# The first feed-forward block in two passes: two of its three token chunks by seven block products in place of eight

## The chip, the cores and the metric

The kernel runs on one core of a Trainium2 chip. The time is the device time of one execution in microseconds, and the figure for a kernel is the median of several runs. A profile is one further execution with the hardware profiler on.

Engines are called as in the profile: PE (matrix products; PEld is its weight load), DVE (vector), ACT (scalar and activations), POOL (general), SP (here only a queue of transfers). Each takes its instructions in program order and waits on semaphores of the others.

## What is computed

One layer of a decoder: a half-step feed-forward block, a mixer of two head groups, and a second feed-forward block. The change touches the first feed-forward block and what joins it to the mixer's projection.

```python
D_MODEL, SEQ, N_META, D_FF = 1024, 1024, 16, 2816

def swiglu(h, w_in, w_out):
    gu = h @ w_in
    g, u = jnp.split(gu, 2, axis=-1)
    return (jax.nn.silu(g) * u) @ w_out

h = h + 0.5 * swiglu(rms_norm(h, ffn1_norm), ffn1_w_in, ffn1_w_out)
u = rms_norm(h, mix_norm) @ w_in
...
h = h + 0.5 * swiglu(rms_norm(h, ffn2_norm), ffn2_w_in, ffn2_w_out)
```

Sixteen meta tokens stand ahead of the 1024 real ones, so the first block has 1040 tokens; the second has 1024.

## The kernel before

**Products.** Everything is float32. To use the fast float32r format, each operand is split into a high part (a cast on ACT: `wh`, `xh`, `ah`, `th`) and a low part (the remainder, a subtraction on DVE or POOL: `wl`, `xl`, `al`, `tl`). Each product of a 128x128 weight tile then takes three PE instructions: high by high, low weight by high, high weight by low.

**The first block** (`ffn`). Tokens are cut into three chunks (`THIRDS`: 352, 344, 344 columns). There are 22 tiles of 128 hidden columns. For each, `stage_in` loads two column tiles of `ffn1_w_in`, splits them, and for each chunk makes `g` and `u` (24 PE instructions each), the gate on ACT (L248), the product on DVE (L249), and its halves `ah` (ACT, L251) and `al` (POOL, L253). `stage_out` takes two hidden tiles at a time, four at the end, and adds their part of the output to `hT` in SBUF (L269). Weights are thus split once for all three chunks, and activations never leave SBUF. Row tiles of x are loaded twice: for the norm (`first_norm`, L622 transposes) and for `hT` (`first_h`). The next norm is made chunk by chunk as `hT` gets ready (`norm_sum`, `inv_rms_rows`, `spread_rows`, `norm_chunk`, from `hooks`). Four projections of the mixer, k and v of the first two chunks, are made at the end beside the norm of the third (`project_early`); k and v of the third follow in `sb_project`.

**The second block** works already in two passes by seven block products, on two chunks of 512 tokens. `fast_in` makes the first pass: for each pair of hidden tiles a "quad" for the gate and one for the other half. A quad multiplies a 2x2 array of weight blocks (128 columns by 512 rows each) with a 2x2 array of token blocks (`B11`, `B21`, `B22`, `T1` to `T4`, made once). The weight combinations are four sums per quad on POOL (L367), and each of the seven weight operands is cast on ACT (L352) and its remainder made on DVE (L354), in three buffers. Results are put together on eviction, and the activations, with their own combinations (POOL, L480, L487), are stored in memory. `fast_out` makes the second pass: for each of seven block products in turn, 11 steps of a weight block of 128x512 and an activation block, both loaded, combined on DVE where needed (L548 to L558) and split (L534, L536), twelve PE instructions each (L582).

**Order.** On PE the order is that of the code (`manual_schedule`). On the other engines and on the queues a scheduler orders instructions by their place in the code and by what they wait for. A tile waits for the last reader of the buffer that it takes.

## Time and profile before

| | us |
|---|---|
| median of 3 runs | 2216.79 (2215.99 to 2218.63) |
| the profiled execution | 2215.04 |
| its span, first to last instruction | 2213.3 |
| first block: first product, last product | 24.1, 813.6 |
| second block, first pass: first and last `qa` | 1547.3, 1973.2 |
| second block, second pass: first and last `o` | 1984.3, 2203.9 |

The page gives busy time by engine, the span in 40 slices, the chain that ended last and the costliest groups. Durations of PE instructions overlap, so the pace of PE is read from starts, or from a count in a stretch of time.

### The profile page before, as it was taken

What the parts mean: (1) busy time and instruction counts of PE and PEld (TensorE: products, weight loads), DVE (VectorE), ACT (ScalarE), POOL (GpSimd) and SP (SyncE); (2) the same over time, 40 slices, a digit from 0 to 9 for tenths busy, and PEclk for the clock granted to TensorE, in tenths of its full rate; (3) what the DMA queues carried; (4) which work ended last, traced back from release to release, by engine and by line L of the source; (5) the groups of instructions that cost most, each with busy time, mean ns of one, the idle gap of its engine ahead of it and who ended that gap; (6) DMA issues with size and microseconds to landing.
All of it is one profiled execution on the core that took longest, in us unless ns stands there. A gap on an engine that the chain in (4) does not pass through costs nothing.

```text
span 2213.3 us, 30720 instructions
## 1 busy us (share of the span) xinstructions
PE 2118.8 (96%) x11916; PEld 1909.2 (86%) x11916; DVE 1179.8 (53%) x1735; ACT 739.1 (33%) x1469; POOL 536.6 (24%) x562
## 2 busy tenths in 40 slices
PE   5999999999999999999999998899899999999999
PEld 4999999999999998997878777787678888878887
DVE  4333223333233163335666659667876767666774
ACT  6311121111211244345555540313423333333443
POOL 1000110011101241233323325211364545440000
PEclk9999999999999999999999999999999999999999
DMA  5311111111111123733433243234533333348363
GB/s 163 106 39 57 39 48 48 39 58 39 57 39 48 46 80 128 208 119 112 123 108 115 87 160 119 73 101 138 160 121 100 106 94 108 97 152 292 112 201 134
DMA packets 215470, 231.08 MB, mean 104 GB/s; under 512 B 18236, under 2 KB 163260, under 8 KB 214812
## 3 DMA queue, kind: packets, MB, share of 16 engines
q1 hardware_dynamic: 203388, 200.47, 29.0%
q0 software_dynamic: 7440, 24.39, 2.9%
q10 hardware_dynamic: 4496, 4.27, 0.6%
q8 instruction: 94, 1.54, 0.3%
q14 instruction: 52, 0.43, 0.1%
HBM read 168.74 MB, written 60.33 MB: 103 GB/s over the span
## 4 chain that ended last, share of the span: by engine, by line
PE 40%; DVE 6%; issue 2%; ACT 2%; POOL 1%; DMA 1%; SPq 0%; DVEq 0%; POOLq 0%; ACTq 0%
PE o L582 9%; PE qb L393 8%; PE qc L393 5%; PE qa L393 5%; PE lvl L779 2%; PE wo L163 1%; PE wo L164 1%; PE wo L162 1%; PE proj L162 1%; DVE keep L1130 1%; PE proj L163 1%; PE proj L164 1%; PE flip L987 1%; DVE attn L788 1%; POOL sig L1133 1%
## 5 line engine op out<-in xcount | busy, mean ns | idle before, releaser
L253 POOL TENSOR_TENSOR al<-sg,ah 128x344 fp32r<-128x344 f32 (+1 forms) x66 | 78.4, 1188 | 655.9 <-ACT ah L251 655.9
L149 DVE TENSOR_TENSOR wl<-raw,wh 128x1024 fp32r<-128x1024 f32 (+1 forms) x112 | 130.7, 1176 | 169.3 <-ACT wh L147 168.0
L147 ACT CAST wh<-raw 128x1024 fp32r<-128x1024 f32 (+1 forms) x112 | 109.4, 986 | 305.8 <-PE o L267 189.0
L162 PE MATMUL proj<-xh,wh 128*128 128x344 f32 (+2 forms) x576 | 205.9, 357 | 1.5 <-ACT wh L147 1.5
L163 PE MATMUL proj<-xh,wl 128*128 128x344 f32 (+2 forms) x576 | 201.1, 349 | 0.8 <-DVE wl L149 0.8
L164 PE MATMUL proj<-xl,wh 128*128 128x344 f32 (+2 forms) x576 | 200.3, 348 | 0.0
L249 DVE TENSOR_TENSOR sg<-sg,u 128x344 f32<-128x344 f32 (+1 forms) x66 | 34.0, 515 | 286.9 <-PE u L164 286.9
L393 PE MATMUL qb<-T,wh 128*128 128x512 f32 x528 | 176.2, 395 | 6.7 <-ACT T L301 3.7
L269 DVE SCALAR_TENSOR_TENSOR hT<-o,hT 128x344 f32<-128x344 f32 (+1 forms) x240 | 123.4, 518 | 101.0 <-PE o L267 101.0
L162 PE MATMUL g<-xh,wh 128*128 128x344 f32 (+1 forms) x528 | 171.5, 325 | 0.0
L163 PE MATMUL g<-xh,wl 128*128 128x344 f32 (+1 forms) x528 | 170.9, 324 | 0.0
L265 PE MATMUL o<-ah,wh 128*128 128x344 f32 (+1 forms) x528 | 170.6, 323 | 0.0
L267 PE MATMUL o<-al,wh 128*128 128x344 f32 (+1 forms) x528 | 170.5, 323 | 0.0
L164 PE MATMUL g<-xl,wh 128*128 128x344 f32 (+1 forms) x528 | 170.1, 322 | 0.0
L266 PE MATMUL o<-ah,wl 128*128 128x344 f32 (+1 forms) x528 | 170.1, 322 | 0.0
L163 PE MATMUL u<-xh,wl 128*128 128x344 f32 (+1 forms) x528 | 169.7, 321 | 0.0
L162 PE MATMUL u<-xh,wh 128*128 128x344 f32 (+1 forms) x528 | 169.4, 321 | 0.0
L164 PE MATMUL u<-xl,wh 128*128 128x344 f32 (+1 forms) x528 | 169.1, 320 | 0.0
L354 DVE TENSOR_TENSOR wl<-s,wh 128x512 fp32r<-128x512 f32 x88 | 123.1, 1400 | 43.1 <-ACT wh L352 42.3
L393 PEld LDWEIGHTS qb<-T,wh 128*128 128x128 f32 x528 | 100.1, 190 | 31.6 <-ACT T L301 4.1
L1133 POOL TENSOR_TENSOR sig<-sig,keep 128x144 f32<-128x144 f32 (+3 forms) x64 | 80.1, 1252 | 178.0 <-DVE keep L1130 114.1
L582 PE MATMUL o<-tl,wh 128*128 128x512 f32 x308 | 120.3, 392 | 2.9 <-DVE tl L536 2.9
(291 smaller groups left out, 5249.7 us busy)
## 6 DMA issues: line engine op xcount, KB each, us to landing
raw<-in_ffn_w_in_dram SPq DMA_DIRECT2D x96, 256.0 KB, 3.0
raw<-in_ffn_w_in_dram SPq DMA_DIRECT2D x44, 512.0 KB, 3.6
raw<-in_ffn_w_out_dram SPq DMA_DIRECT2D x66, 256.0 KB, 4.6
raw<-in_w_in_dram SPq DMA_DIRECT2D x30, 512.0 KB, 3.6
raw<-in_ffn_w_out_dram SPq DMA_DIRECT2D x22, 512.0 KB, 3.6
ks<-kD SPq DMA_DIRECT2D x32, 260.0 KB, 4.6
row<-in_x_dram SPq DMA_DIRECT2D x10, 512.0 KB, 5.1
vD<-vhl SPq DMA_DIRECT2D x8, 512.0 KB, 4.8
```

The costliest lines, as they stand in the source:

```text
L147: nc.scalar.copy(hi, raw)
L149: nc.vector.tensor_sub(lo, raw, hi.bitcast(F32))
L162: nc.tensor.matmul(ps, wh[:, s], xs, start=k == 0, stop=False)
L163: nc.tensor.matmul(ps, wl[:, s], xs, start=False, stop=False)
L164: nc.tensor.matmul(ps, wh[:, s], xl[:, k, c0 : c0 + n], start=False, stop=k == nk - 1)
L265: nc.tensor.matmul(o, wh[:, s], ah, start=i == 0, stop=False)
L266: nc.tensor.matmul(o, wl[:, s], ah, start=False, stop=False)
L267: nc.tensor.matmul(o, wh[:, s], al, start=False, stop=end)
L269: nc.vector.scalar_tensor_tensor(h, o, 0.5, h, ALU.mult, ALU.add)
L354: nc.vector.tensor_sub(lo, src, hi.bitcast(F32))
L393: nc.tensor.matmul(ps, a[:, k, :], b[:, k, :], start=start and k == 0 and i == 0, stop=k == 3 and i == 2, skip_group_check=True,)
L582: nc.tensor.matmul(banks[bank][m], y[:, m * P : (m + 1) * P], z, start=start and q == 0 and e == 0, stop=q == nq - 1 and e == 2, skip_grou ...
```

## The change

The first block now uses `fast_in` and `fast_out` too. Chunks 2 and 1 (344 tokens each) are the two columns of token blocks; chunk 0 (352 tokens) is multiplied plainly.

First pass: for the first three pairs of hidden tiles the plain chunk goes first, 96 PE instructions per pair, while chunks 2 and 1 are loaded (on POOL's queue), normed, transposed and combined (`first_plain`, `first_block`, `first_combined`). Then the seven block products of these three pairs follow, and for the other eight pairs both together: the plain products (`alone`) use weight operands while these are there for the block products, with one operand more (`also`). Between quads two row tiles at a time of x are transposed and stored as `xD` (`turn_x`).

Second pass: 22 steps of the plain chunk with all eight output tiles (`plain_round`), with the loads of `hT` from `xD` after the fourth, then the seven block products. The norm of chunk 0 is spread over the steps of A12 and A11, that of chunk 1 over S3 and A22, that of chunk 2 over A22 and six early projections. `ffn`, `norm_sum`, `norm_chunk`, `first_norm` and `first_h` are gone.

```diff
+    def fast_in(self, ops, n, w_in, actD, openers, ev0, open_ev, feed=None, plain=None,
+                between=lambda: None):
...
+            if also:
+                yield operand(a21)
...
+        def alone(ps, w, h, start):
+            if start:
+                ps = pin.tile([P, n0], F32, tag="qd", name="qd", bufs=2)
+            times(ps, w, plain, 4 * h, start)
+            return ps
+        def plain_quad(col, take):
+            for i in range(2):
+                ps = None
+                for h in range(2):
+                    ps = alone(ps, operand(block(i, h, col)), h, h == 0)
+                take(i, ps)
...
                 p1 = first()
+                if also:
+                    d = alone(None, last[0], 0, True)
                 u2 = kept("u2", p1, go("b", "T2", True))
                 take(0, 0, go("a", "B21", False), None)
+                if also:
+                    also(0, alone(d, last[0], 1, False))
...
+        if plain:
+            for f in ahead:
+                gate, up = plain_pair(f)
+                plain_quad(f * P, gate)
+                yield
+                plain_quad(D_FF + f * P, up)
+                yield
+            ev["p"] = open_ev()
+            for f in ahead:
+                for q in pair(f):
+                    drain(q)
+                    between()
...
+        def plain_round():
+            c0, n0 = plain
...
+            for f in range(D_FF // P):
+                ws = [halved(raw(i, f % 2, f // 2), "w", 512) for i in range(2)]
+                xh, xl = halved(right(f, n0), "t", n0)
+                for m in range(KT):
...
+                if f == 3:
+                    load_h()
+            for m in range(KT):
+                h = hT[:, m, c0 : c0 + n0]
+                nc.vector.scalar_tensor_tensor(h, ps[m], 0.5, h, ALU.mult, ALU.add)
+            ready("plain")
...
+    def first_block(self, ci, rows, junk, pool, name, ops):
...
+        self.norm_rows(ci, rows, junk)
...
+            nc.scalar.mul(t, ps, self.g1[:, k : k + 1])
+            got.append(t)
+            if ops:
+                self.halve(ops[("B11", "B21")[k // 4]], t, k % 4)
...
+                    self.first_plain(rows[0], junk, plain)
+                    next(steps)
+                    next(steps)
+                    ba = self.first_block(2, rows[1], junk, rp, "ba", ops)
+                    next(steps)
+                    next(steps)
+                    bb = self.first_block(1, rows[2], junk, rp, "bb", None)
+                    made = self.first_combined(ba, bb, ops, rp, nw)
...
+                    def load_h():
+                        for k in range(KT):
+                            nc.sync.dma_start(hT[:, k, :], xD[k])
...
+                    self.ring_bufs = 5
...
+                    project_early("k", wk, 0, self.pproj)
+                    project_early("v", wv, 0, pe)
+                    next(last)
+                    project_early("k", wk, 1, self.pproj)
+                    next(last)
+                    project_early("v", wv, 1, pe)
+                    drain(last)
+                    project_early("k", wk, 2, pe)
+                    project_early("v", wv, 2, pe)
```

DVE in the steady part of the first block, before; a row is line, operation, output and inputs, shape, and how often in a row:

```order
L149 TENSOR_TENSOR wl<-raw,wh 128x1024
L249 TENSOR_TENSOR sg<-sg,u 128x352
L249 TENSOR_TENSOR sg<-sg,u 128x344
L149 TENSOR_TENSOR wl<-raw,wh 128x1024
L249 TENSOR_TENSOR sg<-sg,u 128x344
L269 SCALAR_TENSOR_TENSOR hT<-o,hT 128x352
L149 TENSOR_TENSOR wl<-raw,wh 128x1024
L269 SCALAR_TENSOR_TENSOR hT<-o,hT 128x352 x7
L269 SCALAR_TENSOR_TENSOR hT<-o,hT 128x344 x16
```

DVE in the first pass now, in the second quad of a pair that has the plain chunk (`sp` is that chunk's activation, `u` and `sg` those of the block products, `qa` to `qd` PSUM banks):

```order
L397 TENSOR_TENSOR sp<-qd,sp 128x352
L278 TENSOR_TENSOR wl<-raw,wh 128x512
L361 TENSOR_TENSOR u_2353<-qb,p_2265 128x344
L278 TENSOR_TENSOR wl<-s,wh 128x512
L426 TENSOR_TENSOR u<-qc,u_2353 128x344
L427 TENSOR_TENSOR sg<-u,sg 128x344
L278 TENSOR_TENSOR wl<-raw,wh 128x512
L426 TENSOR_TENSOR u<-qb,p_2265 128x344
L427 TENSOR_TENSOR sg<-u,sg 128x344
L278 TENSOR_TENSOR wl<-raw,wh 128x512
```

Each weight remainder is now half as long and serves one or two products of twelve instructions instead of six groups of eight steps; evictions stand between remainders that later products wait for.

DVE in the second pass now, in S1 (`sk` holds the weight combinations of S1 and S2, `raw` a loaded block, `tl` the activation's remainder):

```order
L517 TENSOR_TENSOR tl<-act,th 128x344
L529 TENSOR_TENSOR sk<-raw 128x512
L517 TENSOR_TENSOR wl<-sk,wh 128x512
L532 TENSOR_TENSOR sk<-sk,ak 128x512
L517 TENSOR_TENSOR tl<-act,th 128x344
L517 TENSOR_TENSOR wl<-sk,wh 128x512
L529 TENSOR_TENSOR sk<-raw 128x512
```

Each step of twelve PE instructions has two remainders and a combination here, where the old second half had only the accumulations into `hT`.

SP between the passes now (`act1p` are the plain chunk's stored activations, `xD` the transposed x):

```order
L510 DMA act<-act1p_102 128x352
L283 DMA raw<-in_ffn_w_in_dram 128x4x128
L510 DMA act<-act1p_103 128x352
L283 DMA raw<-in_ffn_w_in_dram 128x4x128 x7
L1387 DMA hT<-xD 128x1040 x8
L505 DMA raw<-in_ffn_w_out_dram 128x512 x6
L510 DMA act<-act1p_104 128x352
```

The eight loads of `hT` stand behind the last weights of the first pass and ahead of the second weight block of the fifth plain step.

More of the change, by code (lines that the diff above doesn't have):

```diff
@@ L347, in fast_in @@
         ev = {}
-        made_yet = {"B11", "B21"}
+        made_yet = {"B11", "B21"} if feed else set(ops)
+        n0 = plain[0].shape[2] if plain else 0
         def operand(src):
@@ L368, in made, with weights @@
             return t
[L370 removed]
+        def weights(col, opened, also):
             if opened:
@@ L586, in fast_out @@
                     )
-                if a == "A12" and q == 3:
-                    for j2 in range(2):
-                        for m in range(KT):
-                            s = slice(cs[j2], cs[j2] + n)
-                            nc.sync.dma_start(hT[:, m, s], self.h2D[m, :, s])
+                if a == "A12" and q == 3 and not plain:
+                    load_h()
+                between(a, q)
             for m in range(4):
@@ L676, in store_out, with project @@
                 nc.sync.dma_start(self.out[0, r0 : r0 + P, 512 * q : 512 * q + 512], row)
-    def project(self, xh, xl, col, chunks, use, keep=0, early=()):
-        for ci in early:
-            use(early[ci], ci, *chunks[ci])
-        w = self.col_tile(self.a["w_in"][0], col)
-        def steps(part):
-            for ci, (c0, n) in part:
-                ps = self.pproj.tile([P, n], F32, tag="proj", name="proj")
-                for half in range(2):
-                    self.product(ps, w, xh, xl, c0, n, range(4 * half, 4 * half + 4))
-                    if half == 0:
-                        yield 12 * n * 0.42
-                use(ps, ci, c0, n)
-                yield 12 * n * 0.42
-        at = list(enumerate(chunks))
-        cut = len(at) - keep
-        yield from steps(at[len(early) : cut])
-        return steps(at[cut:])
+    def project(self, xh, xl, col, chunks, use, w=None):
+        w = w or self.col_tile(self.a["w_in"][0], col)
+        for ci, (c0, n) in enumerate(chunks):
+            ps = self.pproj.tile([P, n], F32, tag="proj", name="proj")
+            for half in range(2):
+                self.product(ps, w, xh, xl, c0, n, range(4 * half, 4 * half + 4))
+                if half == 0:
+                    yield 12 * n * 0.42
+            use(ps, ci, c0, n)
+            yield 12 * n * 0.42
     def hgrn_fill(self, xh, xl, pool, dst):
@@ L1266, in run @@
                 xl = px.tile([P, KT, T], F32R, name="xl")
-                with ExitStack() as c2:
-                    self.weights("w1", 3, 5, c2)
+                with tc.manual_schedule(engines={nc.tensor.engine}), ExitStack() as c2:
+                    self.ring = self.pool("ring1", ctx=c2, side="right")
+                    self.parts = self.pool("parts1", ctx=c2, side="right")
+                    pn = self.pool("norm", ctx=c2)
                     ph = self.pool("h1", ctx=c2)
-                    act = self.pool("act1", ctx=c2)
-                    pin_ctx = ExitStack()
-                    pin = self.pool("pin1", 4, PSUM, pin_ctx)
+                    op_ctx = ExitStack()
+                    self.op = self.pool("op1", ctx=op_ctx)
@@ new lines, in between @@
+                    def between(step, q):
+                        if step in ("A12", "A11", "S1"):
+                            for _ in range(2 if step == "A12" and q < 4 else 1):
+                                next(norms[0], None)
+                        elif step == "S3" and 6 <= q < 10:
+                            if q == 6:
+                                norms[1] = norm_steps(1, banks_of("y"), both, 2)
+                            next(norms[1])
+                        elif step == "A22":
+                            if q == 0:
+                                norms[2] = norm_steps(2, lambda: [(self.pn, "nps")] * 2, both, 1)
+                            for _ in range(2):
+                                next(norms[1], None)
+                            if 6 <= q < 10:
+                                next(norms[2])
+                            if q in (5, 7):
+                                col = {5: 2560, 7: 3072}[q]
+                                early_w.append(self.col_tile(a["w_in"][0], col))
@@ L1393, in run @@
                 (q, x): self.dram.tile([P, n], F32, name=f"act{q}{x}")
-                for q in range(D_FF // 256) for x in ("B11", "B21", "B22", "T1", "T2", "T3", "T4")
+                for q in pairs for x in names
             }
```

438 lines of the change are left out of this document (241 added, 197 removed).

## Prediction

> **What bounds the kernel now.** I read the busy table and the slices first, then stretches of the span, then TensorE's own waits.
>
> ```profile
> span 2213.3 us, 30720 instructions
> PE 2118.8 (96%) x11916; PEld 1909.2 (86%) x11916; DVE 1179.8 (53%) x1735; ACT 739.1 (33%) x1469; POOL 536.6 (24%) x562
> PE   5999999999999999999999998899899999999999
> PEclk9999999999999999999999999999999999999999
> ```
>
> TensorE is busy 96% of the span at full clock, so an operation taken from it may shorten the span, if the stage it leaves is bound by it. The next rows show stretches: length, then busy time and instructions of PE, PEld, DVE, ACT and POOL, then clock, DMA share and GB/s. The first three are the first feed-forward block (start, steady part, end). The last two are the second block, which already works by seven products: its first pass and its second.
>
> ```profile
> 24.00:100.00 76.00, 67.93 (x413) 63.91 (x412) 29.26 (x62) 39.10 (x72) 6.33 (x10) 0.91 0.41 128
> 100.00:750.00 650.00, 650.00 (x4098) 650.00 (x4097) 209.13 (x332) 109.84 (x174) 71.03 (x59) 1.00 0.16 48
> 750.00:814.00 64.00, 62.50 (x394) 62.24 (x393) 31.12 (x68) 22.82 (x50) 21.87 (x22) 0.97 0.22 75
> 1650.00:1950.00 300.00, 300.00 (x1310) 245.44 (x1309) 207.65 (x222) 94.20 (x156) 147.44 (x144) 1.00 0.32 103
> 2000.00:2150.00 150.00, 150.00 (x663) 124.22 (x662) 109.68 (x176) 62.88 (x110) 0.00 (x0) 1.00 0.62 202
> ```
>
> In the steady part of the first block nothing but TensorE matters: 650 of 650 us, VectorE at 32%. In the second block TensorE is still busy throughout, but VectorE is at 69 and 73%. Waits say the same (line, who is waited for, total, times, longest): one row for 1600 to 1950 us, and in the first block little after its start.
>
> ```profile
> PE qb L393 <- DVE u L420: 1.9, 2, 1.0
> ...
> PE xps L622 <- DVE row L636: 9.0, 5, 4.4
> PE nps L187 <- DVE nacc L177: 1.5, 1, 1.5
> ```
>
> A busy TensorE hides its pace, so I take that from starts. The rows are the first and the last of twelve consecutive 344-column products.
>
> ```profile
> 811.90 0.32 PE L265 MATMUL o<-ah,wh 128*128 128x344 f32 x1
> ...
> 813.63 0.32 PE L267 MATMUL o<-al,wh 128*128 128x344 f32 x1
> ```
>
> 1.73 us over 11 steps is **0.157 us a product**; the steady part gives 650/4098 = 0.159 with its 352-column third and the transposes.
>
> **The change, part by part.** *Removed products.* Before, each of the two 344-token chunks has 22 x 2 x 24 = 1056 products in the first pass and 22 x 24 = 528 in the second, together 3168. By seven block products it is 11 pairs x 2 x 84 = 1848 and 7 x 11 x 12 = 924, together 2772. The plain chunk keeps its 1584, and transposes stay at 144. 396 products x 0.157 = **-62.3 us**, from a stage where TensorE's time is the span's.
>
> The Trainium skill, "TensorE: Matmul & The Clock Gate", section "Wait — 56ns, not 53.3ns?", gives a warm product N/2.4 GHz plus about 2.5 ns, an estimate of 0.146 us at 344 columns; the removed products would then be worth 57.7 us. The 0.157 us measured above differs and decides.
>
> *The opening.* The first product starts here:
>
> ```profile
> 24.06 0.64 PE L162 MATMUL g<-xh,wh 128*128 128x352 f32 x1
> ...
> 5.39 1.28 ACT L633 ACT_TABLE_LOAD   x1 [5.39 <-DMA row<-in_x_dram]
> 6.69 1.06 ACT L633 ACTIVATE hT<-row 128x1024 f32<-128x1024 f32 x1
> L352 ACT CAST wh<-raw 128x512 fp32r<-128x512 f32 x66 | 40.8, 622 | 92.1 <-PE qc L393 67.9 <-PE qa L393 19.1 <-PE qb L393 4.6
> L251 ACT CAST ah<-sg 128x344 fp32r<-128x344 f32 x44 | 21.0, 476 | 81.4 <-DVE sg L249 81.4
> ```
>
> From there to 100 us the old kernel records 413 products and transposes, 413 x 0.159 = 65.7 us of 76: it loses 10 us. The new one runs 288 plain products and 48 transposes, about 54 us, over the preparation of the other two chunks. ACT's list for that time, by the order of the program, is about 6 squares at 1.25 with their read-out, 8 table loads at 1.28, 25 weight casts at 0.62, 28 casts and 24 scalings of 344 or 352 at 0.48, and 6 gates: near 63 us. It starts some 11 us before the first product, so it would end with TensorE if it never waited; but it does wait, since scalings follow transposes, and casts free buffers. I expect TensorE to lose about 10 us, as before: **0**, between -5 (no loss but the transposes' turns) and +12 (ACT's list is the path).
>
> *Three pairs without the plain chunk.* A half pair is 84 products, 13.2 us. VectorE has 7 weight remainders (wl) and about 7 evictions in it. Next come two wl rows, POOL's sums, one wl that a POOL sequence held up, and VectorE's pitch.
>
> ```profile
> L354 DVE TENSOR_TENSOR wl<-s,wh 128x512 fp32r<-128x512 f32 x88 | 123.1, 1400 | 43.1 <-ACT wh L352 42.3
> L354 DVE TENSOR_TENSOR wl<-raw,wh 128x512 fp32r<-128x512 f32 x66 | 66.9, 1014 | 1.2 <-ACT wh L352 1.2
> L367 POOL TENSOR_TENSOR s<-raw 128x512 f32<-128x512 f32 x44 | 58.1, 1321 | 57.0 <-DVE wl L354 39.9 <-DMA raw<-in_ffn_w_in_dram 15.8 <-POOL s L367 0.2
> ...
> 1718.17 0.62 ACT L352 CAST wh<-s 128x512 fp32r<-128x512 f32 x1
> 1718.83 3.34 DVE L354 TENSOR_TENSOR wl<-s,wh 128x512 fp32r<-128x512 f32 x1 [1.99 <-ACT wh L352]
> 1719.07 1.30 POOL L480 TENSOR_TENSOR t<-sg,t 128x512 f32<-128x512 f32 x1
> 1720.31 1.30 POOL L487 TENSOR_TENSOR sg<-sg 128x512 f32<-128x512 f32 x1
> ...
> 2058.58 0.68 DVE L536 TENSOR_TENSOR wl<-sk,wh 128x512 fp32r<-128x512 f32 x1
> 2059.18 0.68 DVE L555 TENSOR_TENSOR raw<-raw,sk 128x512 f32<-128x512 f32 x1
> ...
> 779.42 0.53 DVE L177 TENSOR_TENSOR nacc<-nacc,nsq 128x352 f32<-128x352 f32 x1 [0.94 <-ACT nsq L175]
> 779.86 0.51 DVE L269 SCALAR_TENSOR_TENSOR hT<-o,hT 128x344 f32<-128x344 f32 x1
> ...
> 813.00 1.50 DVE L269 SCALAR_TENSOR_TENSOR hT<-o,hT 128x344 f32<-128x344 f32 x3
> ```
>
> Back to back VectorE takes 0.60 us at 512 and 0.44 (from SBUF) or 0.50 us (from PSUM) at 344; starts count, not durations. Beside POOL a remainder takes 1.0 to 1.4. So a half pair is 4 x 1.4 + 3 x 1.0 + 7 x 0.48 = 12.0 of 13.2 us: TensorE still ends last, with nothing to spare. Per pair I allow 1 us for a remainder held as above: **+3** for three pairs; 0 if none is on the path, +12 if each of the six half pairs has 2 us more. Pairs with the plain chunk have 132 products, 21 us, against about 13.5 of VectorE: 0. Storing and reloading activations, the x transposes through memory and POOL's issues lie under this; the second block does as much at a 32% DMA share with no wait.
>
> *Between the passes.* Operands of the first four plain steps are loaded and split ahead, and the ring lies in free room: 1 us (the second block's hand-over waits 3.6 us). The eight loads of h (4.26 MB) stand on SP ahead of the fifth plain step's second weight block. DMA rates at full load:
>
> ```profile
> 2000.00:2010.00 10.00, 10.00 (x46) 8.27 (x45) 4.69 (x8) 3.70 (x7) 0.00 (x0) 1.00 0.95 320
> 2035.00:2045.00 10.00, 10.00 (x46) 8.29 (x45) 7.79 (x14) 3.78 (x7) 0.00 (x0) 1.00 0.90 296
> ```
>
> At 310 GB/s h takes 13.7 us, plus about 2 to land and split; four plain steps cover 4 x 24 x 0.16 = 15.4 us: a wait of 1 to 2 us. Together **+3**, 0 to +8.
>
> *The second pass by blocks.* One step of 12 products is 1.89 us, where the second block's is 2.7. VectorE needs 0.60 + 0.44 for two remainders, in four of the seven products 0.60 more to combine weights, and 4 x 0.50 every 11 steps. That is 11 x 1.64 + 2.0 = 20.0 of 20.8 us in those four. Up to S3, with the norm of chunk 0 and the plain evictions, I count 120 of TensorE's 125 us; in A22, with a norm and two w_in tiles, 23.6 of 20.8. In S1, loads are 11 x (2 x 262 + 176) KB = 7.7 MB, 24.8 us at 310 GB/s against 20.8, part of it loaded ahead in five buffers. I take 3 us for S1's loads, 3 for VectorE's order between S1 and S3 and 3 for A22: **+9**. The bounds are 0 (everything runs ahead) and +22, the sum if each VectorE instruction costs its whole duration (0.69, 0.51).
>
> *The end.* The old end waits at the norm sums and near the last early projections:
>
> ```profile
> PE nps L187 <- DVE nacc L177: 2.8, 2, 1.5
> PE proj L162 <- ACT wh L147: 1.5, 1, 1.5
> ...
> 830.00:840.00 10.00, 7.69 (x38) 7.16 (x37) 3.41 (x3) 3.39 (x6) 0.70 (x1) 0.83 0.36 104
> ```
>
> The new end puts four projections of 24 products (15 us) over the last chunk's norm: **-3**, between -6 (those waits and the thin stretch go) and +4 (the third chunk's projections now wait for the norm's remainders). After it the program is as before.
>
> *Sum.* -62.3 + 0 + 3 + 3 + 9 - 3 = -50.3. The profiled execution took 2215.0 us around its span of 2213.3, so 2164.7; the median of the runs shown is 1.8 higher, so **2166 us**.
>
> **Rivals.** (1) *Cover is nearly whole*: the second block's first pass shows 1.9 us of waits in 350, and the extra terms stay near 5: -62 + 5 - 3 = about 2154. Against it: steps are 30% shorter and VectorE's work per step is not.
>
> (2) *VectorE and ACT become the bound wherever the plain chunk is not there to cover*: opening +8, the three pairs +10, second pass +20, between +4, end 0: -62 + 42 = about 2197. For it: 12.0 of 13.2 and 23.6 of 20.8 us above. Against it: the pitch of 0.60, which is what the long lists are made of. The Trainium skill, "SBUF — State Buffer", section "Who interferes with whom", says that a VectorE instruction with two SBUF inputs and a GpSimd instruction that reads SBUF exclude each other for a whole instruction; the 3.34 us remainder over two POOL sums agrees. That rule makes the three pairs the first place where this rival would show.
>
> (3) *Slower*: the weight operands' chain in the first pass sets the pace. An operand has three buffers, so cast and remainder have to be done within the other two operands' products, 3.8 us, where the second block leaves 5.4. The rows show 0.62 + 1.4 = 2.0 on average and 4.0 at worst. Over some 170 operands each microsecond beyond 3.8 costs 170/3 = 57 us; from a mean of 4.9 the gain is gone, and 5.2 us would give about 2234. Against it: the mean is half of that, and in most pairs two or three operands serve 24 products each.
>
> (4) *The change doesn't remove what it says*: the order has 10289 rows on TensorE for 10688, 399 fewer, so this is out.
>
> **How the numbers follow.** Forecast (2156 to 2178) 0.62; rival 1 0.15; rival 2 0.18 (up to 2205); rival 3 0.04; no change 0.01. The range takes in rival 1 and most of rival 2: 2150 to 2193. The median of few runs scatters by about 0.1%, and 0.2% (4.4 us) is about what can be told from no change. Faster 0.95, same 0.01, slower 0.04.
>
> **What would show it.** Right: some 396 fewer products at 0.157 us; stretches of the first pass with the plain chunk wholly busy, at 0.158 a product; second pass starting near 515 us and the last block product near 760 in place of 814; small waits on wl in the first three pairs and on wl, tl or loads in S1 to A22. The opening's term is wrong if the third set of plain products ends far from 88 us. Wrong altogether: TensorE waiting on wh or wl in most pairs (rival 3), VectorE busy without a gap through S1 to A22 with TensorE below 90% (rival 2), or a hole of many microseconds at the first act load or at h.

## Result, and the profile after

| | before | after |
|---|---|---|
| median, us (4 runs each, beside each other) | 2217.71 (2215.99 to 2221.59) | 2163.36 (2161.26 to 2164.35) |
| ratio to before, 95% interval | | 0.9751 [0.9734, 0.9768] |
| profiled execution, its span | 2215.04, 2213.3 | 2161.26, 2159.5 |
| first product of the first block | 24.1 | 20.6 |
| last block product of its second pass | 813.6 | 759.5 |
| first `z` product of the mixer | 999.2 | 943.9 |

The kernel is 54 us faster. The forecast was 2166. From the page of the changed kernel:

```profile
span 2159.5 us, 32075 instructions
PE 2053.0 (95%) x11520; PEld 1838.6 (85%) x11520; DVE 1384.6 (64%) x2058; ACT 892.5 (41%) x1809; POOL 701.7 (32%) x764
PE   6899999999999999999999987899899999999998
PEclk9999999999999999999999999999999999999999
```

TensorE has 396 instructions fewer and VectorE 323 more. The same three stretches as before, and one of S1 and S2, two of the block products (length; busy time and instructions of PE, PEld, DVE, ACT, POOL; clock, DMA share, GB/s):

```profile
24.00:100.00 76.00, 67.25 (x399) 64.36 (x398) 52.45 (x110) 52.93 (x102) 17.45 (x23) 0.93 0.46 140
100.00:750.00 650.00, 637.84 (x4031) 633.45 (x4031) 410.48 (x663) 267.30 (x515) 240.16 (x261) 0.99 0.50 157
750.00:814.00 64.00, 61.51 (x366) 56.52 (x365) 32.85 (x59) 23.38 (x50) 15.77 (x18) 1.00 0.26 86
...
660.00:680.00 20.00, 19.87 (x126) 19.35 (x125) 19.97 (x38) 11.34 (x23) 0.00 (x0) 1.00 0.65 197
```

Where TensorE was busy 650 of 650 us it now is 638: about 12 us of stops have come in, and in 650 us its clock is below 1.00. The last row is worth a second look. VectorE is busy 19.97 of 20 us, and TensorE 19.87: here an engine is full and holds nobody up. So I looked for TensorE's stops one by one. Its time line holds every stop of 0.7 us or more between the first block product and the second pass's end (start, us, tile, and in brackets the stop and what ended it):

```profile
86.03 0.66 PE L319 MATMUL qa<-B,wl 128*128 128x344 f32 x1 [3.79 <-DVE wl L278]
127.00 0.39 PE L319 MATMUL qb<-T,wh 128*128 128x344 f32 x1 [1.56 <-DVE u L361]
156.17 0.39 PE L319 MATMUL qb<-T,wh 128*128 128x344 f32 x1 [1.57 <-DVE u L361]
441.21 0.40 PE L319 MATMUL qb<-T,wh 128*128 128x344 f32 x1 [0.80 <-DVE u L361]
447.48 0.39 PE L319 MATMUL qb<-T,wh 128*128 128x344 f32 x1 [2.25 <-DVE u L361]
517.98 0.33 PE L553 MATMUL o<-th,wh 128*128 128x352 f32 x1
536.34 0.43 PE L553 MATMUL o<-th,wh 128*128 128x352 f32 x1 [0.96 <-ACT wh L515]
735.38 0.62 PE L586 MATMUL o<-th,wh 128*128 128x344 f32 x1 [4.05 <-DVE hT L596]
759.55 0.32 PE L586 MATMUL o<-tl,wh 128*128 128x344 f32 x1
```

The rows without a bracket are the second pass's first product, with no stop at the hand-over, and its last. The two large stops cost more than themselves. This is the clock behind them, in stretches of 4 us (the clock is the third number from the end):

```profile
84.00:88.00 4.00, 1.97 (x7) 1.97 (x8) 3.19 (x7) 0.36 (x1) 0.54 (x1) 0.59 0.70 234
88.00:92.00 4.00, 4.00 (x17) 4.00 (x16) 0.69 (x1) 0.96 (x2) 0.63 (x1) 0.56 0.84 234
92.00:96.00 4.00, 4.00 (x27) 4.00 (x26) 2.67 (x3) 1.59 (x3) 3.23 (x3) 1.00 0.47 146
...
732.00:736.00 4.00, 0.62 (x2) 0.65 (x3) 2.42 (x5) 3.06 (x6) 0.47 (x1) 0.66 0.60 189
736.00:740.00 4.00, 4.00 (x16) 4.00 (x15) 4.00 (x8) 2.18 (x6) 3.03 (x6) 0.50 0.71 238
```

At a clock of 0.5, TensorE does 16 or 17 instructions in 4 us in place of 27. Each of the two stretches at 0.5 lasts 6.8 us, from 84.7 and from 733.3 us. Their first 1.3 and 2.1 us lie in the stop itself, where TensorE does nothing anyway; the rest costs half its length, 2.8 and 2.4 us. So 3.79 became 6.5, and 4.05 became 6.4. Nothing is lost behind the stops of 1.56, 1.57 and 2.25.

What held the rows up is seen on the other engines. For 86 us, VectorE:

```profile
79.69 2.70 DVE L222 TENSOR_TENSOR T<-ba,T 128x344 fp32r<-128x344 f32 x2
...
85.31 0.68 DVE L278 TENSOR_TENSOR wl<-raw,wh 128x512 fp32r<-128x512 f32 x1
```

VectorE has no gap from 73.6 to 86.5 us. Its list there holds the remainders of the token blocks (`T`, `B`), and the weight remainder that TensorE waits for stands behind them. The two remainders of the first row took 2.70 us beside GpSimd's weight sums, where two others of the same shape took 0.93 at 82.74; how much of the stop this makes was not tested. For 127 us, VectorE and GpSimd:

```profile
122.69 3.74 DVE L278 TENSOR_TENSOR wl<-raw,wh 128x512 fp32r<-128x512 f32 x1 [0.74 <-ACT wh L276]
126.35 0.50 DVE L361 TENSOR_TENSOR u<-qb,p 128x344 f32<-128x344 f32 x1
...
122.46 1.31 POOL L291 TENSOR_TENSOR s<-raw,s 128x512 f32<-128x512 f32 x1
123.71 0.94 POOL L442 TENSOR_TENSOR t<-sg,t 128x344 f32<-128x344 f32 x1
124.59 1.28 POOL L291 TENSOR_TENSOR s<-raw 128x512 f32<-128x512 f32 x1
```

A remainder that takes 0.68 us alone took 3.74: it stood beside three GpSimd sums and ended 0.56 us after the last of them, and the eviction of `qb` stood behind it. For 735 us, ScalarE and VectorE:

```profile
732.50 1.04 ACT L147 CAST wh<-raw 128x1024 fp32r<-128x1024 f32 x1 [4.03 <-DMA raw<-in_w_in_dram]
...
733.58 1.23 DVE L149 TENSOR_TENSOR wl<-raw,wh 128x1024 fp32r<-128x1024 f32 x1 [4.39 <-ACT wh L147]
734.72 1.77 DVE L596 SCALAR_TENSOR_TENSOR hT<-o,hT 128x344 f32<-128x344 f32 x4
```

ScalarE waited 4.03 us for the load of the first early tile of the input projection's weights. VectorE's remainder of that tile stood behind it, and S3's eviction, which A22 needs, behind that. The early tile itself is used 25 us later.

### The profile page after: what moved, and what is told of

It is laid out like the page before. It is cut to its first block, busy times and chain, and to the rows that moved or that the text cites. A ratio compares the mean times of both kernels' runs of the same rounds, so it can differ in the third digit from the quotient of the medians.

```text
span 2159.5 us, 32075 instructions
## 1 busy us (share of the span) xinstructions
PE 2053.0 (95%) x11520; PEld 1838.6 (85%) x11520; DVE 1384.6 (64%) x2058; ACT 892.5 (41%) x1809; POOL 701.7 (32%) x764
## 4 chain that ended last, share of the span: by engine, by line
PE 41%; DVE 6%; issue 2%; ACT 2%; POOL 1%; DMA 1%; SPq 0%; DVEq 0%; POOLq 0%; ACTq 0%
PE o L586 9%; PE qb L319 8%; PE qc L319 5%; PE qa L319 5%; PE lvl L827 2%; PE wo L163 1%; PE wo L164 1%; PE wo L162 1%; PE proj L162 1%; DVE keep L1179 1%; PE proj L163 1%; PE proj L164 1%; PE flip L1036 1%; DMA vT<-hg_v 1%; POOL sig L1182 1%
## 5 line engine op out<-in xcount | busy, mean ns | idle before, releaser
L319 PE MATMUL qb<-T,wh 128*128 128x344 f32 (+1 forms) x1056 | 312.7, 359 | 14.2 <-DVE u L361 10.3
L586 PE MATMUL o<-th,wh 128*128 128x344 f32 (+1 forms) x616 | 218.5, 356 | 4.0 <-DVE hT L596 4.0
L586 PE MATMUL o<-tl,wh 128*128 128x344 f32 (+1 forms) x616 | 218.5, 356 | 3.4 <-DVE tl L517 3.4
L586 PE MATMUL o<-th,wl 128*128 128x344 f32 (+1 forms) x616 | 218.3, 356 | 0.9 <-DVE wl L517 0.7
L319 PE MATMUL qa<-B,wh 128*128 128x344 f32 (+1 forms) x704 | 210.2, 363 | 0.0
L278 DVE TENSOR_TENSOR wl<-raw,wh 128x512 fp32r<-128x512 f32 x172 | 152.2, 888 | 71.8 <-ACT wh L276 67.9
L319 PE MATMUL qb<-T,wl 128*128 128x344 f32 (+1 forms) x528 | 188.7, 357 | 0.0
L319 PE MATMUL qd<-X,wh 128*128 128x352 f32 x704 | 181.8, 326 | 0.0
L319 PEld LDWEIGHTS qa<-B,wh 128*128 128x128 f32 x704 | 129.5, 190 | 16.0
L319 PE MATMUL qa<-B,wl 128*128 128x344 f32 (+1 forms) x352 | 127.0, 361 | 4.0 <-DVE wl L278 4.0
```

The lines of the kernel that those rows point to most:

```text
L278: nc.vector.tensor_sub(lo, src, hi.bitcast(F32))
L319: nc.tensor.matmul(ps, a[:, k, :], b[:, k0 + k, :], start=start and k == 0 and i == 0, stop=k == 3 and i == 2, skip_group_check=True,)
L586: nc.tensor.matmul(banks[bank][m], y[:, m * P : (m + 1) * P], z, start=start and q == 0 and e == 0, stop=q == nq - 1 and e == 2, skip_grou ...
```

## Experiments

Theory: TensorE still sets the pace; what the new form loses are a few single stops, each from one engine's order, with the clock behind the longer ones. Rivals: VectorE is the bound without the plain chunk; or the weight operands' chain is. Twelve runs followed, each beside the kernel before; one of them is the changed kernel again.

| kernel | median us | ratio to before | start to hand-over | plain round | block part |
|---|---|---|---|---|---|
| changed kernel | 2163.4 | 0.9751 [0.9734, 0.9768] | 497.3 | 85.9 | 155.7 |
| again, beside the split on GpSimd | 2162.9 | 0.9749 [0.9731, 0.9767] | 496.2 | 85.8 | 155.6 |
| eighth product put back | 2227.3 | 1.0035 [1.0021, 1.0049] | 539.0 | 85.5 | 174.1 |
| no activation combinations on GpSimd | 2156.8 | 0.9728 [0.9714, 0.9743] | 491.0 | 84.7 | 156.0 |
| two operand buffers | 2172.7 | 0.9791 [0.9774, 0.9808] | 503.4 | 85.9 | 154.8 |
| second pass's sums on GpSimd | 2176.2 | 0.9814 [0.9799, 0.9829] | 497.0 | 85.8 | 165.9 |
| early tiles asked for later | 2160.6 | 0.9735 [0.9722, 0.9748] | 496.1 | 85.9 | 153.2 |
| second pass split after the first | 2169.5 | 0.9772 [0.9758, 0.9785] | 493.1 | 95.4 | 158.1 |
| both of these | 2163.3 | 0.9755 [0.9733, 0.9777] | 492.3 | 94.0 | 154.4 |
| four opening pairs | 2161.0 | 0.9727 [0.9713, 0.9741] | 489.6 | 86.0 | 152.9 |
| early tiles split on GpSimd | 2168.9 | 0.9769 [0.9754, 0.9784] | 497.2 | 86.0 | 156.9 |
| four pairs, split on GpSimd | 2163.6 | 0.9744 [0.9728, 0.9761] | 490.2 | 85.9 | 158.3 |
| four pairs, early load | 2167.2 | 0.9771 [0.9758, 0.9784] | 492.7 | 90.2 | 154.9 |

The three stage columns are us of the profiled execution: first plain product to the second pass's first product; from there to its first block product; from there to its last. Two kernels compute something else than the reference: the one with the eighth product counts two products double, and the one without activation combinations multiplies other data.

### The eighth product put back

```diff
+                if plain and op == "B22":
+                    times(ps[bank], left, ops[op], 0, False)
...
+                if plain and a == "S2":
+                    order = order + order
```

> This kernel adds the eighth product back without any of the old structure: in each of the 22 quads of the first pass of the first block the B22 products are issued twice (264 products), and in each quad of the second pass's block part the S2 steps are issued twice (132 products), so the output counts these two products double. It is 396 products of 344 columns more than in the changed kernel. Theory (TensorE sets the pace in both passes, 0.157 us a product): +62 us over the changed kernel, about 2225 us, +41 of it between the first block product and the second pass's start (436 to about 477 us) and +21 in the block part of the second pass (156 to about 177 us). Against the kernel before it would then be about 8 us slower, and these 8 us are the price of the restructuring. Rival (VectorE or the operands' chain is the bound in the stretches without the plain chunk): the added products hide partly beside it, the second pass's block part grows by under 15 us, the whole by under 50 us, and the kernel is no slower than the kernel before.

Measured: 1.0035 less 0.9751 is 0.0284 of 2218, **63 us**, give or take 5 by the two intervals, for 62.3 forecast by 0.157. The stage to the hand-over grew by 41.7, for 41.4 by 0.157. The block part grew by 18.4, with a smaller stop at S3's eviction:

```profile
560.06 0.33 PE L555 MATMUL o<-th,wh 128*128 128x352 f32 x1
795.70 0.55 PE L590 MATMUL o<-th,wh 128*128 128x344 f32 x1 [2.58 <-DVE hT L600]
819.71 0.32 PE L590 MATMUL o<-tl,wh 128*128 128x344 f32 x1
```

The stop is 1.5 us shorter than 4.05 and cost 1.7 us of clock for 2.4; without that difference the 132 products took 18.4 + 2.1 = 20.5 us, for 20.7 forecast. TensorE is the bound in the first pass and in S2, where VectorE has no gap (20.8 of 20.8 us busy in the changed kernel); the rival is out there. The other steps of the block part had nothing added. And the price of the restructuring stands alone here: 0.35% of 2218, **7.8 us** (4.7 to 10.9), where the forecast's terms beside the removed products came to 12.

### GpSimd's activation combinations left out

```diff
+                if plain:
+                    for x, t in (("T1", (0, 1)), ("T2", (1, 1)), ("T3", (0, 1)), ("T4", (1, 0))):
+                        put(x, sg[t])
+                    return
```

> This kernel leaves out the four combinations of the activations (T1 to T4) that GpSimd adds up in the first pass of the first block; the quarters themselves are stored in their place, so the block products are of other data and as many. Theory: the waits of 1.56 and 1.57 us at the starts of the second and third pair (127 and 156 us in the changed kernel's trace) come from a VectorE remainder held up beside GpSimd's combinations; without them these two waits go, and the first pass is 2 to 4 us shorter (436 to 432 to 434 us). Rival: these waits belong to the order in which VectorE takes the pair's halvings, whatever GpSimd does; then they stay within 0.3 us of their size, and the first pass stays within 1 us. The wait of 0.66 us at 86 us (behind the halving of T4 and B22) goes by both, or shrinks, since VectorE has less ahead of it.

Measured: the stage to the hand-over is 6.3 us shorter, more than expected, and the stops at 127 and 156 us are gone. So are those at 441 and 447. Between the first block product and the hand-over these of 0.4 us or more remain:

```profile
85.39 0.66 PE L319 MATMUL qa<-B,wl 128*128 128x344 f32 x1 [3.75 <-DVE wl L278]
109.40 0.42 PE L319 MATMUL qc<-T,wh 128*128 128x344 f32 x1 [0.82 <-ACT wh L276]
112.62 0.40 PE L319 MATMUL qb<-T,wh 128*128 128x344 f32 x1 [0.49 <-DVE u L361]
```

The hold-up by GpSimd's sums is shown. The expectation for 86 us failed: 3.75 us stayed (I had read the row's second number, the instruction's 0.66 us, as the stop), so VectorE's backlog there does not come from these sums. GpSimd's weight sums are still in this kernel.

### Two operand buffers in place of three

```diff
-            hi = wp.tile([P, 4, P], F32R, tag="wh", name="wh", bufs=3)
+            hi = wp.tile([P, 4, P], F32R, tag="wh", name="wh", bufs=2 if plain else 3)
```

(and `lo` likewise)

> The first pass of the first block has two buffers in place of three for the halves of its weight operands. It tests the prediction's slower rival (a weight operand must be made within 3.8 us of its buffer coming free, and each us beyond costs 57 us over the 170 operands). Theory that three buffers leave the chain wide room: two buffers still leave room in most quads, waits of 0.3 to 1 us appear at some operands, and the first pass is 3 to 25 us longer than 436 us. Rival (the chain was near its limit with three): with two, each operand waits some 1 to 2 us and the first pass is 60 to 110 us longer. A third reading, that the chain has no part in the pace at all, gives under 2 us.

Measured: 6.1 us more to the hand-over, 9 us on the medians. From the first block product to the hand-over, the stretch that the expectation counts, it is 438.2 for 436.1, so only 2 us more: less than the theory's 3, and close to the third reading. The new stops lie before 131 us, but for one of 0.53 at 488:

```profile
84.50 0.43 PE L319 MATMUL qd<-X,wl 128*128 128x352 f32 x1 [2.16 <-DVE wl L278]
88.95 0.43 PE L319 MATMUL qa<-B,wl 128*128 128x344 f32 x1 [2.27 <-DVE wl L278]
...
115.60 0.42 PE L319 MATMUL qc<-T,wh 128*128 128x344 f32 x1 [2.08 <-ACT wh L276]
```

The four stops at 127, 156, 441 and 447 us do not appear in this kernel; why was not followed. Even with one buffer fewer, most of the 170 operands cost nothing. With three, the chain of the prediction's slower rival was far from its limit.

### The second pass's sums on GpSimd

```diff
-                nc.vector.tensor_add(s, raw(1, 0, q), raw(1, 1, q))
+                (nc.gpsimd if plain else nc.vector).tensor_add(s, raw(1, 0, q), raw(1, 1, q))
...
-                sub(s, s, a)
+                (nc.gpsimd.tensor_sub if plain else sub)(s, s, a)
```

> The second pass's sums of weight blocks that VectorE makes in the block part (S1's addition and S2's subtraction, of 128x512 elements each) are made on GpSimd instead. Theory: VectorE is busy 95 to 100 per cent there without holding TensorE up, since what it does late is not what TensorE waits for; taking two operations a quad off it changes the block part by no more than 2 us, and if anything makes it longer, since a GpSimd sum beside a dense VectorE stretch took 7.00 us where 0.9 is usual, and an operand that is late by that stops TensorE for 1 to 5 us: 156 to between 155 and 175 us. Rival (VectorE near its bound is what the block part loses 8 us to): 3 to 8 us shorter.

Measured: the block part is 10 us longer. S1's sums run ahead of it, beside A11's products, and there GpSimd's sums and VectorE's remainders hold each other up (a remainder `tl` takes 0.50 us alone):

```profile
623.43 2.98 POOL L529 TENSOR_TENSOR sk<-raw 128x512 f32<-128x512 f32 x1 [2.82 <-DMA raw<-in_ffn_w_out_dram]
...
629.45 1.57 DVE L517 TENSOR_TENSOR tl<-act,th 128x344 fp32r<-128x344 f32 x1
...
629.58 0.43 PE L586 MATMUL o<-th,wl 128*128 128x344 f32 x1 [1.60 <-DVE wl L517]
631.08 0.59 PE L586 MATMUL o<-tl,wh 128*128 128x344 f32 x1 [1.07 <-DVE tl L517]
```

Taking work off a full VectorE this way made TensorE wait more. By itself that doesn't show that VectorE's load was harmless, since the sums on GpSimd also made VectorE's own rows longer; the eighth product in S2 does.

### Early tiles later; second pass split after the first; both

```diff
-                            if q in (5, 7):
-                                col = {5: 2560, 7: 3072}[q]
+                            if q in (8, 9):
+                                col = {8: 2560, 9: 3072}[q]
```

> The two early tiles of the input projection's weights are taken up at the ninth and tenth quad of the second pass's last products in place of the sixth and eighth. Theory: the wait of 4.05 us at 735 us in the changed kernel (ScalarE's copy of the early tile waits for its load, VectorE's remainder stands behind it, and S3's eviction behind that), with the lower clock of 0.83 that follows it, goes: the block part of the second pass is 4 to 6 us shorter (156 to 150 to 152 us). A wait may come back at the projection's first products, of 0 to 4 us; the whole is 1 to 6 us shorter than the changed kernel. Rival (the eviction is late for another cause, GpSimd's 7 us sum at 721 us or VectorE's own backlog): a wait of 3 to 5 us stays at the same place in the order, and the time is the same.

Measured: the stop fell to 1.86, but not by the edit. In the order of ScalarE's instructions the first early tile's copy kept its place; only the second tile's moved, by one weight block, and it stood behind the stop in both kernels. Why the scheduler left the first where it was is not known. What differed was the load's landing, 1.84 us after ScalarE was ready in place of 4.03:

```profile
728.86 1.05 ACT L147 CAST wh<-raw 128x1024 fp32r<-128x1024 f32 x1 [1.84 <-DMA raw<-in_w_in_dram]
```

So this kernel is close to a repeat of the changed one, and the mechanism had yet to be tested by taking the load away. Its size can be tested already: in all ten traces where ScalarE's copy waits for this load, TensorE's stop is that wait and 0.01 to 0.02 us more, from 1.84 and 1.86 here to 4.76 and 4.78 in the next kernel.

```diff
-                    self.parts = self.pool("parts1", ctx=c2, side="right")
+                    self.parts = self.pool("parts1", ctx=c2)
```

> The second pass's first weight operands are split only when the first pass has ended (their pool lies where the first pass's lay, and not beside it). Theory: the waits of 0.80 and 2.25 us at 441 and 447 us go, since no copy that waits for a load stands in the tenth pair's order; in their place TensorE stops at the hand-over, where it now stops for nothing, by 1.5 to 4 us. The whole is within 2 us of the changed kernel. Rival (the two waits at 441 and 447 come from the tenth pair's own combinations, as at 127 and 156 us): they stay, the hand-over's stop comes on top, and the kernel is 2 to 4 us slower.

Measured: the stops at 441 and 447 are gone and the hand-over comes 4 us earlier, but the plain round takes 95.4 us in place of 85.9, and the median is 6 us higher, with intervals that overlap:

```profile
515.52 0.43 PE L553 MATMUL o<-th,wl 128*128 128x352 f32 x1 [1.05 <-DVE wl L517]
518.07 0.66 PE L553 MATMUL o<-tl,wh 128*128 128x352 f32 x1 [2.12 <-DVE tl L517]
538.50 0.43 PE L553 MATMUL o<-th,wh 128*128 128x352 f32 x1 [2.74 <-ACT wh L515]
```

Two edits that have nothing in common, this one and leaving out GpSimd's activation combinations, each remove the stops at 441 and 447, so both the early splits and GpSimd's sums seem to be needed for them; with two operand buffers they are gone as well, which this does not explain. The price at the hand-over was underestimated, since two stops so close cost 2.7 us of clock, and the third 1.7.

> Both moves together: the early tiles of the input projection at the ninth and tenth quad, and the second pass's first operands split after the first pass. Theory: the effects lie some 290 us apart and add up: 2 to 6 us shorter than the changed kernel, some 2158 to 2161 us. Rival: the later splits only move the waits and the late tiles bring a wait at the projection: the same time within 2 us.

Measured: 2163.3, the rival's figure; since the later tiles did nothing to the first copy's place, it is the split alone once more (plain round 94.0), with an early tile that happened to land sooner (ScalarE waited 2.63 us).

### Four opening pairs

```diff
-                        ops, nw, a["ffn1_w_in"][0], act1D, 3, ev0, open_ev, None, plain, between
+                        ops, nw, a["ffn1_w_in"][0], act1D, 4, ev0, open_ev, None, plain, between
...
-                    for _ in range(2):
+                    for _ in range(4):
```

> Four pairs of row blocks open the first pass without the plain chunk in place of three, so the plain chunk's products begin one pair later. Theory: the wait of 0.66 us at 86 us stays (it depends on the first pair's halvings), a third hold-up like those at 127 and 156 us (1.57 us) appears at the fourth pair's start, and the first pass is 1 to 3 us longer. Rival (the stretches without the plain chunk are short of VectorE, GpSimd or the weight operands' chain): a fourth such pair costs 5 us or more.

Measured: neither. The stop at 86 us went, a third hold-up of 1.5 us came, and the stage to the hand-over is 7.7 us shorter. The same two stretches of 4 us as above, in this kernel:

```profile
84.00:88.00 4.00, 4.00 (x27) 4.00 (x26) 1.38 (x2) 1.59 (x3) 0.00 (x0) 1.00 0.75 218
88.00:92.00 4.00, 4.00 (x27) 4.00 (x26) 1.63 (x3) 1.69 (x4) 2.62 (x2) 1.00 0.84 269
```

No stop, no clock lost: 6.5 us saved, less 1.6 for the added hold-up; one stop of 1.98 us in the tenth pair stands for two of 3.05 together, and the opening's stops are 0.7 us shorter. That comes to 6.7 of the 7.7. The preparation has one more pair of plain products to run beside, and VectorE is busy 10.5 of the 12.9 us from 73.6, where it had no gap. Yet the span was 2160.2 and the changed kernel's 2159.5. The first `z` came at 933.5, 10.5 us earlier, and the rest took 1226.8 us in place of 1215.6. The sum of (1 - clock) over the rest is 23.0 us in place of 11.7: the whole difference. Why this execution lost more clock there is not known.

### Again, and the early tiles' split on GpSimd

> The changed kernel once more, unaltered, beside the next two on one chip. Earlier runs show its profiled execution between 1.7 us steps of lost clock: after the first z product that execution lost 11.6 us to a lower granted clock, and eight others of nearly the same program 16 to 23. Expected: 2163 us within 3, the stops at 86 us (3.8 us) and near 735 us (2 to 4 us, as far as the early tile's load lands late) again, and 15 to 20 us of lost clock after the first z, so a span of 2160 to 2166.

Measured: 2162.9, with stops of 3.76 and 3.87 us in the same two places. This profiled execution lost 18.0 us of clock behind the first `z`, and took 1220.9 us for that rest: the same program as the changed kernel, whose execution lost 11.7 and took 1215.6.

```diff
-            nc.vector.tensor_copy(hi, raw)
+            (nc.gpsimd if self.split_on_vector == "pool" else nc.vector).tensor_copy(hi, raw)
...
-                            self.weights("we", 2, 2, c2)
+                            self.weights("we", 2, 2, c2, on_vector="pool")
```

(and the remainder likewise)

> GpSimd makes both halves of the two early tiles of the input projection's weights, in place of ScalarE's copy and VectorE's remainder. Nothing in ScalarE's or VectorE's order ahead of S3's eviction then waits for that load. Theory: the stop at the first A22 product (4.05 us in the changed kernel, 1.9 to 4.8 in its variants) goes to under 0.6 us, and with it the half-clock stretch behind it (1.7 or 3.4 us): the second pass is 4 to 7 us shorter (241.6 to 235 to 238 us). The whole 3 to 7 us shorter than the control. Rival (the eviction is late because VectorE's backlog at 95 to 100 per cent busy is): a stop of 2 us or more stays there. Second rival: GpSimd's copy of 128x1024 delays the norm's sums and the stop only moves behind A22, with the same time.

Measured: the stop at the first A22 product is gone: with the wait's size above, its cause is shown. The second rival came true: other stops stand in A22 (VectorE, GpSimd, TensorE), and the median is 6 us above the control's, with intervals that overlap.

```profile
732.38 2.89 DVE L517 TENSOR_TENSOR wl<-raw,wh 128x512 fp32r<-128x512 f32 x1
...
737.79 1.32 DVE L210 TENSOR_TENSOR nacc<-nacc,nsq 128x344 f32<-128x344 f32 x1 [1.37 <-POOL nacc L210]
...
732.17 2.55 POOL L149 TENSOR_TENSOR wl<-raw,wh 128x1024 fp32r<-128x1024 f32 x1
...
739.77 0.42 PE L586 MATMUL o<-th,wl 128*128 128x344 f32 x1 [2.30 <-DVE wl L517]
748.64 0.90 PE L198 MATMUL spread<-diag,ones_d 128*128 128x128 f32 x6 [1.34 <-DVE diag L195]
```

The first row, held beside GpSimd's remainder, stopped TensorE for only 0.47 us. The stop of 2.30 comes from the second row: VectorE's norm sum waited for one that GpSimd makes behind its remainder, and the weight remainder that TensorE needed stood behind that.

> The early tiles split on GpSimd and four opening pairs in place of three. Theory: the stop of 3.79 us at 86 us with its lower clock (1.7 or 3.4 us) and the stop at the first A22 product with its own are both gone, one hold-up of 1.57 us is added: the first block ends 8 to 14 us before the control's, and the whole is 5 to 14 us shorter, some 2150 to 2158 us, with less stopped time left to lose clock by. Rival (what the first block wins is lost again to a lower clock behind it, as in the run with four pairs alone, whose first block ended 10 us earlier and whose end did not come earlier): the same time as the control within 3 us.

Measured: 2163.6, the rival's figure, but by another road. The hand-over is 6 us earlier, as with four pairs alone, and the block part is 2.6 us longer than in the changed kernel: two stops of 1.84 and 1.70 us in A22, with 13.7 us at half the clock from the first one on.

### Four pairs and an early load

```diff
+                    pr = self.pool("early_raw", ctx=c2)
-                    self.ring_bufs = 5
+                    self.ring_bufs = 4
...
+                        elif step == "S1":
+                            kept.append(load_early(2560))
```

> Four opening pairs in place of three, and the raw data of the first early tile of the input projection's weights in a buffer of its own that is loaded when S1's products end, some 70 us ahead of S3's eviction; the second early tile uses the same buffer after it, so its copy no longer stands ahead of that eviction. The ring of weight blocks of the second pass has four buffers in place of five, which makes the room. Theory: with no load in ScalarE's and VectorE's order ahead of the eviction, the stop at the first A22 product (1.9 to 4.8 us so far) goes to under 0.6 us and nothing takes its place, as GpSimd's sums are not beside 128x1024 remainders of its own; the block part of the second pass (155.9 us in the changed kernel) is 147 to 151 us, and the first block ends 10 to 16 us before the control's 758 us. The whole: 2163 less 5 to 14, some 2150 to 2158 us. Rival: VectorE's full order at that place stops TensorE by 1 to 4 us somewhere in A22 whatever is taken out of it, as with the split on GpSimd; the block part stays at 153 us or more, and the time within 5 us of the control. Third: four ring buffers are too few and each step waits for its blocks; the second pass is then 5 us or more longer.

Measured: with the load out of the way no stop at all stands at the first A22 product, the second proof of its cause. But in the plain round ScalarE now waits 5.66 us for a weight block, which fits the shorter ring, and a norm sum in A22 is late:

```profile
531.62 0.66 PE L560 MATMUL o<-th,wh 128*128 128x352 f32 x1 [2.89 <-ACT wh L522]
744.95 0.90 PE L205 MATMUL spread<-diag,ones_d 128*128 128x128 f32 x6 [1.69 <-DVE diag L202]
```

Against the changed kernel the block part gained 0.8 us and the plain round lost 4.3; against four pairs alone both are longer, by 2.0 and 4.2. The kernel is no better. No version beats the changed kernel for certain: four opening pairs are lowest of those that compute the reference, 0.9727 for 0.9751 and 0.9749, and the intervals overlap.

## Why the prediction was right

The two profiled executions give a ledger. A stretch's idle time is its length less TensorE's busy time; its lost clock is half of the busy time that TensorE spent at a granted clock of 0.50. What is left is the products' own time.

| us | before | now | change | forecast |
|---|---|---|---|---|
| start to the first product | 24.1 | 20.6 | -3.4 | in the opening |
| opening (to 92.2; to 81.9), idle + lost clock | 8.1 + 5.9 | 5.0 + 1.7 | -7.3 | 0 |
| from there to the hand-over (before: to 780) | 0 | 10.0 + 2.8 | +12.7 | +3 |
| plain round | | 1.3 | +1.3 | +3 |
| block part (before: from 780) | 1.5 + 1.7 | 4.7 + 2.4 | +3.9 | +9, and part of -3 |
| products and transposes themselves | 772.4 | 711.2 | -61.2 | -62.3 |
| last block product to the first `z` | 185.5 | 184.4 | -1.1 | part of -3 |
| behind the first `z` | 1214.1 | 1215.6 | +1.4 | 0 |
| span | 2213.3 | 2159.5 | -53.8 | -50.3 |

- **Removed products, -62.3.** Right: 61.2 by the ledger, and 63, give or take 5, by putting them back.
- **The opening, 0.** The first block product came at 81.9 and not near 88. With the earlier first product the opening is 10.7 us better, outside the bound of -5. The old opening lost 14.0 us and not 10: I had priced its 120 transposes like products, and in the new first pass transposes start only 0.11 us apart. The new one lost 6.7 and not as much as before. Why its first product comes 3.4 us earlier was not followed.
- **Three pairs without the plain chunk, +3.** The mechanism was right (a remainder held by GpSimd's sums), and its size: 1.56 + 1.57 in the second and third pair. The step that failed is its bound to those pairs' steady work. At the first pair's start TensorE met VectorE's backlog of remainders from the preparation, 3.79 us with 2.8 of clock; and two more stops, 3.05 us, came in the tenth pair, which I had put at nothing since the plain chunk covers it.
- **Between the passes, +3.** 1.3 us, at the loads of `hT` (0.96 and 0.29), and no stop at the hand-over. By the forecast's own numbers the wait at the loads was 13.7 + 2 - 15.4 = 0.3 us, and not the 1 to 2 it took.
- **The second pass by blocks, +9.** 7.1, so the size was nearly right and the reason was not. I took 3 us for S1's loads, 3 for VectorE's order from S1 to S3 and 3 for A22. VectorE was as full as I had counted, 118.5 of 125.2 us up to S3's end, but that cost 0.49 us, in A11; there was no wait for loads, and A22's own steps cost nothing. In their place stands one stop, 4.05 us with 2.4 of clock, from a load that an instruction of the mixer waited for.
- **The end, -3.** -1.1 from the last block product to the first `z`, and the old norm's stop at 800 us, 1.5 with 1.7 of clock, is gone: -4.3.
- Behind the first `z` I had left the time unchanged; it grew by 1.4.

That the total lies within 4 us of the forecast is in part luck: the opening was 10.7 us better than its term, the stretch from the first block product to the hand-over 9.7 us worse. Rival 1 (cover nearly whole) wanted some 5 us of extra terms, and the first pass alone lost 12.7. Rival 2 fell with the eighth product, rival 3 with two buffers.

What the forecast lacked is the clock. It priced a stop at its own length.

## What to carry to other kernels

Price an added stop of TensorE by its length: here 19 of 20 of 2.5 us and more cost 1.5 to 2.9 us on top, 9 of 14 near 2 us cost 1.7 or more, and those of 1.5 to 1.6 at the pairs' starts nothing, so the longest stop is the first to look at. In each engine's order, look for the instruction that waits for a load and does not belong to the current stage; what stands behind it on that engine and the next is what waits. A full engine is a bound only if TensorE's own stops name it; adding TensorE work back and seeing whether it costs its full price settles it.

## What the runs showed of the hardware

**The clock behind a stop.** In the first block, from its first block product on, the thirteen traces of this form have 20 stops of 2.5 to 4.8 us; in or just behind 19 of them the clock fell to 0.50 for 3.4 us or 6.8. Where the fall began within the stop, part of it cost nothing; 1.5 to 2.9 us were lost. Of 14 stops of 1.84 to 2.30 us that stand alone 9 were followed by such a fall, and of 25 of 1.53 to 1.60 us at the pairs' starts none; one of 1.69 in A22 was. Falls come in steps of 3.4 us at half the clock, that is 1.7 us. The same stop of 2.25 or 2.26 us in the tenth pair lost nothing in three traces and 1.7 us in four, so its length alone does not decide. The Trainium skill, "TensorE: Matmul & The Clock Gate", section "What's actually happening", has the clock at one half after an idle window of about 3.4 us, with windows that run freely: the factor and the step agree. The same page of the Trainium skill, section "Why this matters for your kernels", warns of gaps over about 3 us; here gaps of 2 us were often enough. That the phase of the window decides would fit the stop in the tenth pair, but was not tried.

**A part of the scatter.** The losses behind the first `z`, by (1 - clock), were 11.7 to 23.0 us in the thirteen traces of this form, and 11.7 and 18.0 in two of the same program. The gain of a few us of a variant can lie below this in any one execution, as with four opening pairs.

**VectorE and GpSimd.** They hold each other up in both directions. A remainder of 0.68 us took 3.74 beside GpSimd's sums and 2.89 beside GpSimd's remainder. In the changed kernel a GpSimd sum of 128x344, 0.94 us at 123.71, took 7.00: VectorE ran without a gap for the first 6.2 of them, on instructions with two inputs from SBUF, and the sum ended 0.8 us after VectorE's first gap began:

```profile
721.22 7.00 POOL L210 TENSOR_TENSOR nacc<-nacc,nsq 128x344 f32<-128x344 f32 x1 [5.86 <-ACT wh L515]
```

The Trainium skill, "SBUF — State Buffer", section "Who interferes with whom", has the one that issues first keep the shared port for a whole instruction. The long rows agree in kind; that the wait can last over many instructions of the other engine, as in the 7.00 us, is what the trace adds.
